# Spacing the bursts of partial-array products in a list-scheduled encoder layer

## The chip, the cores and the metric

One Trainium2 chip, one core. The metric is the device time of one execution in microseconds (us). The kernel before takes 2392.24 us, the median of 3 runs (2391.76 to 2394.51).

## The reference: what is computed

One layer of a bidirectional encoder, over two sequences (512 and 1024 tokens of 1024 channels), in float32:

```python
h = rms_norm(x, n_pre_mix); proj = h @ w_in            # 6672 columns
# Gated DeltaNet, 4 heads of 128, forward and backward
o_a = gated_delta_chunked(q, k, v, g[0], beta[0]) + flip(gated_delta_chunked(flip(q), ...))
# HGRN2, 4 heads of 128, forward and backward
o_b = gla_chunked(qh, kh[0], ih, logf[0]) + flip(gla_chunked(flip(qh), ...))
y_a = (rms_norm(o_a) * silu(z)) @ w_br_gdn;  y_b = (rms_norm(o_b) * silu(g)) @ w_br_hg
x = x + rms_norm((gates[0] * y_a + gates[1] * y_b) @ w_out, n_post_mix)
h2 = rms_norm(x, n_pre_ffn)
return x + rms_norm((silu(h2 @ w_gate) * (h2 @ w_up)) @ w_down, n_post_ffn)
```

Inside each chunk `gated_delta_chunked` solves a unit lower triangular system. The kernel forms the inverse of its matrix: 32x32 blocks first, then merged to 64x64 and to 128x128 by small products.

## The kernel before, in words

**Dense products.** Every large matrix product is done with 128x128 weights against 128x512 moving data. Each float32 operand is split into a high and a low part, and three products (high by high, high by low, low by high) are added in one PSUM bank. In the trace they are `MATMUL ... 128*128 128x512`, one instruction for the weights and one for the product.

**Partial-array products.** The merges of the triangular inverse (`merges` in `gdn_mix`, below `def pairs`) use quarters and halves of the array: 32x32 and 64x64 weights (`32*32 32x32`, `64*64 64x64` in the trace). They are plain float32, and each one becomes four instructions of the tensor engine: two weight loads and two products, so the trace has two `MATMUL` for one product of the program. For one head of the 1024-token sequence the merges are four bursts: 32 products of 32x32, a copy of their result, 48 products of 32x32, copies, 16 products of 64x64, a copy, 16 products of 64x64. For the 512-token sequence the bursts are half as long. HGRN2 has bursts of its own, with 128x32 weights.

**Who sets the order.** Nothing is issued as it is written. `Tape` records every instruction as an `Op` with a modelled duration (`cost`), `units` joins products of one form that follow each other into a unit (one burst above is one unit), and `schedule` then runs a list scheduler over the whole program: it keeps a modelled clock for each engine, holds a heap `future` of units whose operands come later and a heap `ready` of units that could start, and lets the engine with the earliest possible start take its ready unit of the lowest `prio` (its place in the written order). A unit whose PSUM bank is still read by another engine is put back into `future` with the time `w` at which it may start. `emit` then writes the instructions in the order found. [...] The name `form` is the shape of the weights for float32 products, `FULL` is (128, 128), and it is `None` for the dense products.

All recorded instructions go through one call, so all rows of the profile have the line of `emit` (L632 before, L649 in the changed kernel); the tiles' names tell them apart. `bank` is any PSUM bank; `ha_a` holds the split activations and `wa_a` the split weights of the dense products in the mixer part, `xr_a` those of the later part; `la_a`, `ba_a`, `sm_a` and `sa_a` hold the rest.

**Stages.** Projections, mixers and first part of the feed-forward are interleaved in about the first 1160 us. After that come dense products only.

Of the kernel before, what the change touches and what calls it, by code (L numbers as in the profile page):

```python
# [2 lines left out]

# [42 lines left out]
PO = False  # L46
NVEC = 88
AHEAD = {1: 1536, 3: 2064, 7: 4112 - 512}
TOKENS, NORMED = 14.0, 30.0
QSQ = P * EPS ** 0.5  # L50
EPSQ = P * EPS * EPS
# [109 lines left out]
class Tape:  # L161
# [11 lines left out]
    GROUP = 4  # L173
    AHEAD = 500
    RATE = 260.0
    SLACK = {"sync": 600, "vector": 100, "scalar": 100, "gpsimd": 100, "tensor": 100}

    class Eng:
# [252 lines left out]
    def schedule(self):  # L431


        self.units()
        ops = self.ops
        for o in ops:
            o.succ = []
            o.rel = 0.0
            o.asked = False
        npend = [0] * len(ops)  # L440
        for o in ops:
            for j in o.need:
                if ops[j].unit is not o.unit:
                    npend[o.unit[0].idx] += 1
                    ops[j].succ.append(o)
        pools = []
        for v in self.vts.values():
            if v.ops:
                v.left = len(v.ops)
                v.fin, v.use = {}, {}  # L450
                v.pool.tiles.append(v)
                if v.pool not in pools:
                    pools.append(v.pool)
        for p in pools:
            p.begin(len(ops), self.cuts)
        engs = list(self.ENGS)
        future = {e: [] for e in engs}
        ready = {e: [] for e in engs}
        clock = {e: 0.0 for e in engs}
        lanes = []  # L460
        start, turn = {}, {}
        far = []
        front = 0

        def lat(a, b):
            a, b = self.ENGS[a], self.ENGS[b]
            return self.LAT.get((b, a), 30 if a == b else 36)

        def ask(o):

            if o.idx > front + self.AHEAD:
                heapq.heappush(far, o.idx)
                return
            for x in o.unit:
                for v in x.tiles:
                    if v.at is None:
                        got = v.pool.take(v, front)
                        if got is None:
                            heapq.heappush(v.pool.queue, (o.prio, o.idx))
                            return  # L480
                        v.fin = {}
                        for f in got:
                            for e, t in f.items():
                                v.fin[e] = max(v.fin.get(e, 0.0), t)
                    for e, t in v.fin.items():
                        if v.left == len(v.ops):
                            o.rel = max(o.rel, t + lat(e, x.eng))
            heapq.heappush(future[o.eng], (o.rel, o.idx))

        def enable(o, t):  # L490
            o = o.unit[0]
            npend[o.idx] -= 1
            o.rel = max(o.rel, t)
            if npend[o.idx] == 0:
                ask(o)

        def retry(p):
            q, p.queue = p.queue, []
            while q:
                ask(ops[heapq.heappop(q)[1]])  # L500

        for o in ops:
            if o.unit[0] is o and npend[o.idx] == 0:
                ask(o)
        done = 0
        form = None
        wire = 0.0
        held = {"vector": 0.0, "gpsimd": 0.0}
        while done < len(ops):
            best = None  # L510
            for e in engs:
                t = clock[e]
                fu, re_ = future[e], ready[e]
                while fu and fu[0][0] <= t:
                    i = heapq.heappop(fu)[1]
                    heapq.heappush(re_, (ops[i].prio, i))
                if re_:
                    c = t
                elif fu:
                    c = fu[0][0]  # L520
                else:
                    continue
                if best is None or c < best[0]:
                    best = (c, e)
            assert best is not None, "no instruction can start"
            t, e = best
            fu, re_ = future[e], ready[e]
            while fu and fu[0][0] <= t:
                i = heapq.heappop(fu)[1]
                heapq.heappush(re_, (ops[i].prio, i))  # L530
            k = None
            if e == "tensor" and form == self.FULL:
                k = min((x for x in re_ if ops[x[1]].form == form and x[0] < re_[0][0] + self.NEAR), default=None)
            if k is None:
                k = heapq.heappop(re_)
            else:
                re_.remove(k)
                heapq.heapify(re_)
            o = ops[k[1]]
            w = t  # L540
            for x in o.unit:
                for v in x.tiles:
                    if v.pool.kind == "PSUM":
                        for b, f in v.use.items():
                            if b != e:
                                w = max(w, f + lat(b, e))
            if w > t:
                heapq.heappush(fu, (w, o.idx))
                continue
            if o.meth == "dma_start":  # L550
                if len(lanes) >= self.LANES:
                    t = max(t, lanes[-self.LANES])
                wire = max(wire, t + 1000) + o.form
                o.dur = max(o.dur + o.form, wire + 700 - t)
                lanes.append(t + o.dur)
            if e == "tensor":
                if o.form is not None and o.form != form:
                    t += self.ENTER if o.form == self.FULL else self.SWITCH
                form = o.form
            if o.port:  # L560
                w = max(0.0, held["gpsimd" if e == "vector" else "vector"] - t - o.port)
                o.dur += w
                o.occ += w
                held[e] = t + o.dur
            freed = []
            first = t
            for o in o.unit:
                start[o.idx] = (t, done)
                turn[o.idx] = (first, done)
                for v in o.tiles:  # L570
                    if v.pool.kind == "PSUM":
                        v.use[e] = t + o.dur
                done += 1
                clock[e] = t + o.occ
                fin = t + o.dur
                for s in o.succ:
                    if s.eng == e == "tensor":
                        enable(s, t + o.occ)
                    else:
                        enable(s, fin + lat(e, s.eng) + (self.SLACK[e] if e != s.eng else 0))  # L580
                for v in o.tiles:
                    if v.left == len(v.ops):
                        v.fin = {}
                    v.left -= 1
                    v.fin[e] = max(v.fin.get(e, 0.0), fin)
                    if v.left == 0:
                        v.pool.give(v)
                        if v.pool not in freed:
                            freed.append(v.pool)
                t += o.occ  # L590
            f0 = front
            while front < len(ops) and front in start:
                front += 1
            for p in freed:
                retry(p)
            if front > f0:
                while far and far[0] <= front + self.AHEAD:
                    ask(ops[heapq.heappop(far)])
                for p in pools:
                    if p not in freed and p.queue:  # L600
                        retry(p)
            elif freed:
                for p in pools:
                    if p not in freed and p.queue and any(s.waits for s in p.segs):
                        retry(p)
        self.span = max(clock.values())
        self.start = start
        return [ops[i] for i in sorted(turn, key=turn.get)]
# [139 lines left out]
def layer(ctx, tc, x_p, x_s, w_out, n_post_mix, n_post_ffn, w_down, vec, xt_p, xt_s, w_in, w_br, w_gate, w_up,  # L748
# [304 lines left out]
    def need(*keys):  # L1053
        def f():
            ts_ = [pl.done.get(k) for k in keys]
            return None if None in ts_ else max(ts_)
        return f
# [1169 lines left out]

    def pre_stream():
        yield from prelude(seqs[0])
        yield need(("inv", 0, 2))  # L2230
        yield from prelude(seqs[1])

    def gdn_stream():
# [244 lines left out]
    for _ in range(2):  # L2478
        t = pl.tile(hp, [P, KD * TB], F32R, "ring", "ring", 2)
# [122 lines left out]
```

## Time and profile before

| what | value |
|---|---|
| median of 3 runs | 2392.24 us (2391.76 to 2394.51) |
| the profiled execution's own time | 2393.4 us |
| its span | 2391.7 us |
| mean granted clock of the tensor engine | 0.997 |
| tensor engine, products (PE) | 2368.8 us busy, 99%, 14133 instructions |
| tensor engine, weight loads (PEld) | 1976.9 us busy, 14133 instructions |
| VectorE (DVE), ScalarE (ACT), GpSimd (POOL) | 72%, 52%, 31% busy |
| PE's instruction queue (q8) | 111 packets, 1.82 MB |

How to read it: times are in us from the start of the span. PE's busy time is a union of products whose ends are modelled, so a short gap between two products can stand as busy. What the tensor engine loses is better read from the starts in the timeline. `[2.50 <-issue]` behind a row is idle time ahead of it for which the trace shows no semaphore. In a table of windows, PEclk is the granted clock (1.00 is full speed) and (x11) the number of products that began there.

### The profile page before, as it was taken

To read this page: it belongs to the slowest core of one execution; us is meant where nothing else is said; L and a number is where in the kernel's file an instruction comes from. 1 tells how busy PE (TensorE), PEld (TensorE's weight loads), DVE (VectorE), ACT (ScalarE), POOL (GpSimd) and SP (SyncE) were. 2 spreads that over 40 slices of the span, in tenths; PEclk is the share of its full clock that TensorE was granted. 3 is DMA by queue.
4 is the path that set the end of the run, shared out by engine and by line. 5 is a ranking of instruction groups with operands and counts; after the bars stand their busy time and mean duration, and the time that the engine had idled before them with its cause. 6 is when DMAs were issued, how large, how long until landed. Compare 5 with 4: busy or idle time off the path is not lost.

```text
span 2391.7 us, 37849 instructions
## 1 busy us (share of the span) xinstructions
PE 2368.8 (99%) x14133; PEld 1976.9 (83%) x14133; DVE 1733.5 (72%) x2827; ACT 1241.0 (52%) x2158; POOL 752.6 (31%) x1019
## 2 busy tenths in 40 slices
PE   8999999999999999999999999999999999999998
PEld 6888888878888888888888888888888888888887
DVE  7787899848847959748866894755887878545566
ACT  6665876736636637547442464544353544433343
POOL 0623434231602602502310001113666764200221
PEclk9999999999999999999999999999999999999999
DMA  5241743321320231233874453552454544674463
GB/s 197 90 150 63 240 128 88 98 67 41 107 93 18 91 92 54 77 97 117 297 256 176 141 207 120 174 157 94 165 191 163 189 173 166 202 254 139 148 205 125
DMA packets 193495, 337.72 MB, mean 141 GB/s; under 512 B 53184, under 2 KB 92960, under 8 KB 193312
## 3 DMA queue, kind: packets, MB, share of 16 engines
q1 hardware_dynamic: 193312, 335.31, 42.3%
q8 instruction: 111, 1.82, 0.3%
q14 instruction: 72, 0.59, 0.1%
HBM read 254.59 MB, written 80.66 MB: 140 GB/s over the span
## 4 chain that ended last, share of the span: by engine, by line
PE 95%; DVE 3%; DMA 1%; issue 1%; ACT 0%; SPq 0%; POOL 0%; DVEq 0%; ACTq 0%; POOLq 0%
PE bank L632 95%; DVE la_a L632 1%; DMA la_a<-lay_w_in 1%; DVE ba_a L632 1%; DVE sm_a L632 0%; DVE wa_a L632 0%; SPq L632 0%; ACT wa_a L632 0%; ACT la_a L632 0%; ACT ba_a L632 0%; DMA dram_cr_sc<-sm_a 0%; DVE da_a L632 0%; DMA dram_u_sc<-la_a 0%; POOL sm_a L632 0%; DVE sa_a L632 0%
## 5 line engine op out<-in xcount | busy, mean ns | idle before, releaser
L632 PE MATMUL bank<-ha_a,wa_a 128*128 128x512 f32 x5424 | 1308.4, 395 | 0.1
L632 PEld LDWEIGHTS bank<-ha_a,wa_a 128*128 128x128 f32 x5424 | 1004.2, 188 | 203.4 <-issue 1.6
L632 PE MATMUL bank<-xr_a 128*128 128x512 f32 x1386 | 314.3, 389 | 0.0
L632 PEld LDWEIGHTS bank<-xr_a 128*128 128x128 f32 x1386 | 260.1, 188 | 54.0
L632 PE MATMUL bank<-xr_a,ha_a 128*128 128x512 f32 x1200 | 275.2, 389 | 0.0
L632 PEld LDWEIGHTS bank<-xr_a,ha_a 128*128 128x128 f32 x1200 | 225.2, 188 | 46.8
L632 POOL TENSOR_TENSOR ba_a<-ba_a 128x512 f32<-128x512 f32 (+1 forms) x129 | 168.7, 1315 | 229.4 <-ACT wa_a L632 86.7
L632 ACT ACTIVATE la_a<-la_a 128x512 f32<-128x512 f32 (+1 forms) x303 | 191.4, 648 | 60.5 <-DVE la_a L632 44.4
L632 ACT ACTIVATE wa_a<-la_a 128x1024 fp32r<-128x1024 f32 (+1 forms) x120 | 117.1, 983 | 129.1 <-PE bank L632 117.0
L632 DVE TENSOR_TENSOR wa_a<-la_a,wa_a 128x1024 fp32r<-128x1024 f32 (+1 forms) x120 | 141.8, 1189 | 51.5 <-PE bank L632 33.4
L632 DVE TENSOR_TENSOR wa_a<-ba_a,wa_a 128x1024 fp32r<-128x1024 f32 (+1 forms) x104 | 126.1, 1228 | 71.7 <-PE bank L632 50.4
L632 ACT ACTIVATE ha_a<-ba_a 128x512 fp32r<-128x512 f32 (+1 forms) x123 | 79.2, 646 | 138.5 <-PE bank L632 113.1
L632 POOL TENSOR_TENSOR sm_a<-la_a 128x28 f32<-128x28 f32 (+36 forms) x186 | 86.6, 466 | 203.2 <-DMA la_a<-dram_u_sc 151.6
L632 ACT ACTIVATE wa_a<-ba_a 128x1024 fp32r<-128x1024 f32 (+1 forms) x104 | 100.5, 984 | 85.5 <-PE bank L632 71.9
L632 DVE TENSOR_TENSOR ha_a<-ba_a,ha_a 128x512 fp32r<-128x512 f32 (+1 forms) x123 | 127.3, 1039 | 14.0 <-ACT ha_a L632 13.4
L632 DVE TENSOR_TENSOR la_a<-la_a 128x512 f32<-128x512 f32 (+2 forms) x182 | 125.5, 700 | 9.8 <-ACT la_a L632 8.2
L632 POOL TENSOR_TENSOR la_a<-la_a 128x256 f32<-128x256 f32 (+1 forms) x62 | 66.0, 1076 | 172.5 <-DVE la_a L632 86.6
L632 PE MATMUL bank<-wa_a,ha_a 128*128 128x512 f32 x528 | 120.1, 389 | 0.0
L632 ACT ACTIVATE ba_a<-ba_a 128x512 f32<-128x512 f32 (+1 forms) x172 | 109.9, 647 | 17.8 <-DVE ba_a L632 9.4
L632 DVE TENSOR_TENSOR xr_a<-da_a,xr_a 128x1024 fp32r<-128x1024 f32 (+2 forms) x60 | 71.1, 1199 | 64.1 <-ACT xr_a L632 44.0
L632 PEld LDWEIGHTS bank<-wa_a,ha_a 128*128 128x128 f32 x528 | 99.0, 188 | 20.5
L632 ACT ACTIVATE xr_a<-da_a 128x1024 fp32r<-128x1024 f32 (+2 forms) x60 | 58.6, 987 | 106.0 <-PE bank L632 105.0
(205 smaller groups left out, 3391.7 us busy)
## 6 DMA issues: line engine op xcount, KB each, us to landing
la_a<-lay_w_in SPq DMA_DIRECT2D x69, 512.0 KB
ba_a<-lay_w_in SPq DMA_DIRECT2D x35, 512.0 KB
ba_a<-lay_w_up SPq DMA_DIRECT2D x35, 512.0 KB
ba_a<-lay_w_gate SPq DMA_DIRECT2D x35, 512.0 KB
dram_a_sc<-xa_a SPq DMA_DIRECT2D x56, 256.0 KB
ba_a<-w_ffn_down SPq DMA_DIRECT2D x24, 512.0 KB
da_a<-dram_a_sc SPq DMA_DIRECT2D x22, 512.0 KB
ba_a<-dram_a_sc SPq DMA_DIRECT2D x20, 512.0 KB
```

What stands on the lines that cost most here:

```text
L632: f(*[m(a) for a in o.args], **{k: m(a) for k, a in o.kw.items()})
```

## The change

`schedule` keeps a queue `past` of what the tensor engine has been given: for each instruction group its modelled start and how many instructions it is (4 for a float32 product, 2 for a dense product or a transpose). Before a unit of partial-array products is given out, entries older than `FETCH` (5000 ns) are dropped, and the unit's instructions are added to those that are left. If they come to more than `BLOCK` (256; for a unit that is itself over 192 instructions, its own count and 64), the unit goes back into `future` with the time at which enough of the older entries will have passed out of the 5000 ns. No wait is put into the program: only the order found is another.

```diff
+    FETCH = 5000.0
+    BLOCK = 256
...
+        past = deque()
...
+            if e == "tensor" and o.form is not None and o.form != self.FULL:
+                n = 4 * len(o.unit)
+                while past and past[0][0] < t - self.FETCH:
+                    past.popleft()
+                n += sum(c for _, c in past) - max(self.BLOCK, n + 64)
+                for s, c in past:
+                    if n <= 0:
+                        break
+                    n -= c
+                    w = max(w, s + self.FETCH + 1)
             if w > t:
                 heapq.heappush(fu, (w, o.idx))
                 continue
...
+            if e == "tensor":
+                past.extend((t + i * o.occ, 4 if x.form is not None and x.meth == "matmul" else 2) for i, x in enumerate(o.unit))
...
+TRIG = 2
...
-        yield need(("inv", 0, 2))
+        yield need(("inv", 0, TRIG))
```

The last two hunks put a name in place of a number and change nothing.

The rows below are the tensor engine's order. A row is the line, the instruction, the tiles and the shape of the result, and xN how many products of the program stand in a row. The first place is head 0 of the 1024-token sequence, the end of its burst of 32 products of 32x32 and the start of its burst of 48. Before:

```order
L632 MATMUL bank_88<-la_a 32x32
L632 MATMUL bank_88<-la_a,ba_a 32x32
L632 MATMUL bank_89<-ha_a,wa_a 128x512 x6
L632 MATMUL bank_91<-la_a 32x32 x4
L632 MATMUL bank_93<-la_a 32x32 x2
```

The same place in the changed kernel:

```order
L649 MATMUL bank_88<-la_a 32x32
L649 MATMUL bank_88<-la_a,ba_a 32x32
L649 MATMUL bank_89<-ha_a,wa_a 128x512 x21
L649 MATMUL bank_94<-ha_a,wa_a 128x512
L649 MATMUL bank_91<-la_a 32x32 x4
L649 MATMUL bank_93<-la_a 32x32 x2
```

Between the two bursts stood 6 dense products, and now stand 22. These are the first rows of the tensor engine that differ. Heads 1, 2 and 3 had 5, 5 and 12 there and have 22 now.

The second place is the end of the burst of 48 in the same head and the start of its first 64x64 burst. Before:

```order
L632 MATMUL bank_91<-la_a 32x32 x4
L632 MATMUL bank_93<-la_a 32x32 x2
L632 MATMUL bank_89<-ha_a,wa_a 128x512 x11
L632 MATMUL bank_88<-la_a 64x64
L632 MATMUL bank_88<-la_a,ba_a 64x64
```

In the changed kernel:

```order
L649 MATMUL bank_91<-la_a 32x32 x4
L649 MATMUL bank_93<-la_a 32x32 x2
L649 MATMUL bank_94<-ha_a,wa_a 128x512 x18
L649 MATMUL bank_89<-la_a 64x64
L649 MATMUL bank_89<-la_a,ba_a 64x64
```

Here 11 dense products became 18; in heads 1 to 3 it was 10, 12 and 12 and is 18.

The third place is head 3, where the gap between the bursts of 32 and 48 was the widest before:

```order
L632 MATMUL bank_87<-ha_a,wa_a 128x512 x6
L632 MATMUL bank_90<-la_a 32x32 x32
L632 MATMUL bank_87<-ha_a,wa_a 128x512 x12
L632 MATMUL bank_90<-la_a 32x32 x4
L632 MATMUL bank_88<-la_a 32x32 x2
```

In the changed kernel:

```order
L649 MATMUL bank_90<-ha_a,wa_a 128x512 x6
L649 MATMUL bank_92<-la_a 32x32 x32
L649 MATMUL bank_90<-ha_a,wa_a 128x512 x18
L649 MATMUL bank_88<-ha_a,wa_a 128x512 x4
L649 MATMUL bank_92<-la_a 32x32 x4
L649 MATMUL bank_94<-la_a 32x32 x2
```

The 12 dense products became 22. The number of all products, and of the bursts (48 of them), is the same in both kernels. So is the number of dense products ahead of each 128x32 burst that follows these places: 2036, 2132, 2620, 2751, 3156, 3300, 3758 and 3806, before and after.

More of the change, by code (lines that the diff above doesn't have):

```diff
@@ L1 @@
 import heapq
+from collections import deque
 from contextlib import ExitStack, contextmanager
```

## The prediction

> **What bounds the kernel now.** I read the page first, then who the tensor engine waits for, then its timeline around the bursts, then tables of windows for the clock. The page:
>
> ```profile
> span 2391.7 us, 37849 instructions
> PE 2368.8 (99%) x14133; PEld 1976.9 (83%) x14133; DVE 1733.5 (72%) x2827; ACT 1241.0 (52%) x2158; POOL 752.6 (31%) x1019
> q8 instruction: 111, 1.82, 0.3%
> PE 95%; DVE 3%; DMA 1%; issue 1%; ACT 0%; SPq 0%; POOL 0%; DVEq 0%; ACTq 0%; POOLq 0%
> ```
>
> The products are 99% of the span and 95% of the chain that ended last, so only what shortens the tensor engine's own stream counts. The q8 row is its instruction queue: 1.82 MB in 111 packets is 16.4 KB each, and 2 x 14133 instructions over 111 packets is 255 instructions in each. So the stream comes in blocks of 256. What the engine waits for, over the whole span and then from 505 us on:
>
> ```profile
> PE bank L632 <- ACT la_a L632: 7.9, 2, 7.1
> PE bank L632 <- issue: 5.7, 3, 2.5
> PE bank L632 <- ACT wa_a L632: 1.1, 2, 0.6
> PE bank L632 <- DVE la_a L632: 0.8, 2, 0.5
> ...
> PE bank L632 <- issue: 5.7, 3, 2.5
> PE bank L632 <- ACT la_a L632: 0.8, 1, 0.8
> ```
>
> 7.1 us is the start of the program. The rest is 2.7 us of waits for data (0.8 us of it after 505 us) and three idle times of 5.7 us in all that no semaphore explains. The timeline of PE shows the three, each in the second burst of 32x32 products of a head of the long sequence; the first fence is head 0:
>
> ```profile
> 509.04 0.21 PE L632 MATMUL bank<-la_a 32*32 32x32 f32 x1
> ...
> 509.72 1.66 PE L632 MATMUL bank<-ha_a,wa_a 128*128 128x512 f32 x6
> 511.31 0.70 PE L632 MATMUL bank<-la_a 32*32 32x32 f32 x59
> 514.52 0.53 PE L632 MATMUL bank<-la_a 32*32 32x32 f32 x37 [2.50 <-issue]
> 514.98 4.35 PE L632 MATMUL bank<-ha_a,wa_a 128*128 128x512 f32 x11
> ...
> 664.95 1.42 PE L632 MATMUL bank<-ha_a,wa_a 128*128 128x512 f32 x5
> ...
> 668.57 0.21 PE L632 MATMUL bank<-la_a 32*32 32x32 f32 x1 [1.38 <-issue]
> 668.81 4.10 PE L632 MATMUL bank<-ha_a,wa_a 128*128 128x512 f32 x10
> ...
> 853.72 1.42 PE L632 MATMUL bank<-ha_a,wa_a 128*128 128x512 f32 x5
> ...
> 857.75 0.19 PE L632 MATMUL bank<-ba_a,la_a 32*32 32x32 f32 x1 [1.80 <-issue]
> ```
>
> In head 0 the engine stops in the middle of a burst, after 59 of 96 products, with the same operands before and after. If a block of instructions was missing, the stops must lie a whole number of blocks apart. Two windows from stop to stop:
>
> ```profile
> 514.50:668.50 154.00, 152.68 (x1271) 129.52 (x1271) 126.31 (x246) 96.03 (x182) 54.52 (x93) 0.99 0.27 80
> 668.50:857.70 189.20, 186.54 (x1403) 157.56 (x1404) 136.53 (x256) 103.70 (x198) 56.30 (x101) 0.99 0.22 68
> ```
>
> 1271 products and 1271 loads are 2542 instructions, 18 short of 10 blocks of 256; 1403 and 1404 are 2807, 9 short of 11 blocks. The missing few are semaphore instructions, which the table leaves out. I read the stops as waits for an instruction block. Head 3 has the same bursts and no stop:
>
> ```profile
> 1037.46 0.75 PE L632 MATMUL bank<-la_a 32*32 32x32 f32 x64
> 1038.14 3.02 PE L632 MATMUL bank<-ha_a,wa_a 128*128 128x512 f32 x12
> 1041.09 1.04 PE L632 MATMUL bank<-la_a 32*32 32x32 f32 x96
> ```
>
> There 12 dense products stand between the bursts, not 6 or 5. That is the change's own remedy at a smaller dose.
>
> The stops have a second price, in the granted clock. Windows around the stops (PE busy, then the other engines, granted clock third from the end):
>
> ```profile
> 512.46:515.87 3.41, 1.35 (x41) 1.17 (x42) 0.66 (x2) 0.79 (x1) 1.03 (x4) 1.00 0.20 73
> 515.87:519.29 3.42, 3.42 (x11) 2.18 (x9) 3.29 (x9) 0.02 (x1) 0.00 (x0) 0.50 0.00 0
> ...
> 666.06:669.47 3.41, 2.03 (x101) 1.54 (x100) 1.84 (x4) 1.61 (x3) 0.14 (x2) 1.00 1.04 353
> 669.47:672.89 3.42, 3.42 (x11) 2.18 (x9) 1.89 (x5) 0.00 (x0) 1.27 (x2) 0.50 0.81 175
> 853.79:857.20 3.41, 2.15 (x84) 1.56 (x85) 2.94 (x4) 0.00 (x0) 0.00 (x0) 1.00 0.52 211
> 857.20:860.62 3.42, 2.87 (x28) 2.38 (x28) 2.36 (x6) 1.96 (x3) 0.00 (x0) 1.00 0.30 71
> ```
>
> After a window of 3.41 us with 1.35 us or 2.03 us of products, the next one runs at 0.50; after 2.15 us it does not. The third stop is split over two windows and goes free.
>
> **The change part by part.** *The stops.* The listed idle counts from the modelled end of the product before, so I add one product's length:
>
> ```profile
> L632 PE MATMUL bank<-la_a 32*32 32x32 f32 x608 | 10.8, 196 | 4.1 <-issue 3.9 <-DVE la_a L632 0.3
> ```
>
> 2.50 + 1.38 + 1.80 + 3 x 0.196 = 6.27 us from start to start. Do they all go? The tightest is head 0: from its first burst's start (509.04) to the resumption (514.52) the missing block took 5.48 us. With 22 dense products at 0.227 us,
>
> ```profile
> 84.32 37.67 PE L632 MATMUL bank<-ha_a,wa_a 128*128 128x512 f32 x165
> ```
>
> ((37.67 - 0.39) / 164, with 0.39 us for the last one's length), the same product comes 0.68 (first burst, 509.72 - 509.04) + 22 x 0.227 + 0.11 (head 3's 3.02 us for 12 against 11 x 0.227 + 0.39, rounded) + 0.52 (59 products) = 6.3 us after that start, 0.8 us later than the block. Heads 1 and 2 needed about 4.3 and 4.7 us (668.57 - 664.95 + 0.68; 857.75 - 853.72 + 0.68). So all three go: -6.3 us. Bounds: one still there, 2.7 us; none.
>
> *The clock.* At 0.50 the 11 and 10 dense products took 4.35 and 4.10 us. Head 3's 12 took 3.02; 11 would take 2.79 and 10 would take 2.57. So 1.56 + 1.53 = 3.1 us go with the idle that caused them. Bounds: both stay, 0; both go, -3.1.
>
> [...]
>
> *The dense products moved.* 16, 17, 17 and 10 more stand ahead of the bursts of 48, and 7, 8, 6 and 6 more ahead of the first 64x64 bursts: 87 x 0.227 = 19.7 us of work that is done sooner and lacks later. Nothing is added, and its cover is that other dense products are ready when these are gone. The order says they are: each later 128x32 burst has the same number of dense products ahead of it. So 0 now, 19.7 us if the cover were gone.
>
> *Changes of form.* 48 bursts before and after, so as many entries and exits. Counted in the order, dense products alternate with 128x128 float32 products about 12 times more. Bounds each: 0 to 0.11 us (the return from a burst, above), so 0 to 1.3 us; since these keep the whole array, I take the low end, +0.1.
>
> *Waits for data.* From 505 us on PE waited 0.8 us for data. The new order could take that away or, at worst by the page, bring as much as the whole program had, 2.7 us. VectorE copies each burst's result before the next burst; with 22 dense products between (5.0 us) instead of 6, that copy has more time. The copy's readers, the 64x64 merges and the recurrence behind them, come up to 5 us later in a head; what waits behind them on PE is dense work that does not need them. I take 0.
>
> Sum against the profiled execution (2393.4 us, span 2391.7, 1.7 us outside): -6.3 - 3.1 + 0.1 = -9.3, span 2382.4, execution 2384.1. The median of the runs is 1.2 us under the profiled execution, so I subtract from the median: 2392.2 - 9.3 = **2383 us**, -0.39%.
>
> **The rivals.**
>
> (a) *The clock is not the stops' doing.* Small products fill little of the array, and the slow windows come from the bursts, which stay. For it: both windows hold bursts. Against it: a window full of bursts kept its clock, and so did head 3.
>
> ```profile
> 608.00:611.40 3.40, 3.40 (x138) 2.81 (x137) 3.40 (x7) 2.30 (x5) 2.63 (x6) 1.00 0.15 59
> ```
>
> Time: 2392.2 - 6.3 + 0.1 = 2386. [...]
>
> (b) *One stop returns.* The four extra semaphore instructions and the new order shift the block borders, and one burst meets one, with its slow window: 2383 + 2.7 + 1.5 = 2387. For it: the margin of 0.8 us. Against: the rule spaces by instruction count, wherever the border lies.
>
> (c) *The change doesn't do what it says.* The stops are not waits for instructions and return in the new order at the same products: 2392. Against it stand the whole numbers of blocks and head 3.
> [...]
>
> (d) *Slower.* The 87 dense products are missed later in the mixers: the recurrences of the last head end up to 5 us late, nothing dense is ready, and PE idles. It decides from the point where more than 9.3 us / 0.227 = 41 of them are missed. All 87: 2383 + 19.7 = 2403. Against it: 0.8 us of waits for data in all of the mixers after 505 us, and the unchanged counts ahead of later bursts.
>
> **How the numbers follow.** Forecast, 2381 to 2385.5: 0.65. (a) 0.13. (b) 0.09. (c) 0.08. (d) 0.05. A change under 0.2% (4.8 us) can't be told from none here, so faster means under 2387.4. That takes the forecast, (a) and about half of (b), 0.82; same is the other half of (b), (c) and a little of (d), 0.14; slower 0.04. The range takes in (a) and (b), the bounds of alternation and waits (+1.3, +2.7, -0.8), and leaves (c) and (d) out: 2380 to 2388.5.
>
> **What would show it.** Right: no idle `<-issue` on PE in the second bursts of the four heads; granted clock 1.00 in all windows around them (mean above 0.997); PE busy for about 9 us less; waits for data still 2 to 4 us; 22 and 18 dense products between bursts in the timeline. Clock wrong: slow windows without stops. Stops misread: idle `<-issue` again, not a whole number of blocks apart. Cover wrong: PE waits for DVE or ACT, or for POOL's inverse, between 520 and 1160 us.

## The result, and the profile after

The changed kernel takes 2388.11 us (median of 17 runs, 2385.86 to 2389.97) against 2392.58 for the kernel before beside it (17 runs). The ratio is 0.9982, with a 95% interval of 0.9974 to 0.9989. That is 4.3 us less by the ratio and 4.5 by the medians, where 9.3 were forecast. The direction holds and the interval lies below 1, but the size is under half, and it lies within the 0.2% that the prediction took as not to be told from no change. In the profiled executions it is 2389.0 us against 2393.4, span 2387.3 against 2391.7, so 4.4 us.

The page of the changed kernel, the lines that answer to those shown of before:

```profile
span 2387.3 us, 37828 instructions
PE 2367.1 (99%) x14133; PEld 1975.4 (83%) x14133; DVE 1727.1 (72%) x2827; ACT 1239.1 (52%) x2158; POOL 750.5 (31%) x1019
q8 instruction: 111, 1.82, 0.3%
```

The products and the instruction packets are the same in number. The timeline of PE in head 0 (start, length, then instruction, operands, shapes, count):

```profile
509.86 5.29 PE L649 MATMUL bank<-ha_a,wa_a 128*128 128x512 f32 x22
515.08 1.05 PE L649 MATMUL bank<-la_a 32*32 32x32 f32 x96
516.05 4.38 PE L649 MATMUL bank<-ha_a,wa_a 128*128 128x512 f32 x18
```

There are 22 and 18 dense products around the second burst, and its 96 products run without a break. The same windows of time that held the first stop, and then the half clock:

```profile
512.46:515.87 3.41, 3.41 (x104) 2.67 (x103) 0.36 (x1) 1.14 (x2) 0.85 (x1) 1.00 0.19 77
515.87:519.29 3.42, 3.42 (x40) 2.84 (x27) 3.00 (x8) 3.42 (x6) 0.14 (x2) 1.00 0.02 5
```

Both are full of products, at a granted clock of 1.00. So the two large terms of the forecast were collected. What was given back stands in the list of PE's waits from 505 us on, in which before had 5.7 us of `issue` and 0.8 us of waits for data:

```profile
PE bank L649 <- DVE la_a L649: 1.5, 2, 1.3
PE bank L649 <- ACT la_a L649: 0.9, 1, 0.9
PE bank L649 <- ACT ba_a L649: 0.8, 1, 0.8
PE bank L649 <- ACT wa_a L649: 0.5, 2, 0.2
PE bank L649 <- DVE sm_a L649: 0.2, 1, 0.2
```

`issue` is gone, and 0.8 us of waits for data have become 3.9 us, in seven waits. One of the seven, 0.9 us for ScalarE at 830.30, is the wait that before had at 836.52; the other six are new. A table of windows shows where. First before, then the changed kernel; the second number is the window's length and the third PE's busy time:

```profile
500.00:700.00 200.00, 196.12 (x1667) 165.09 (x1666) 145.93 (x284) 111.93 (x210) 61.51 (x108) 0.98 0.31 90
700.00:900.00 200.00, 197.37 (x1498) 168.31 (x1497) 143.41 (x278) 110.39 (x213) 57.14 (x98) 1.00 0.20 60
900.00:1160.00 260.00, 260.00 (x2021) 220.87 (x2020) 199.80 (x381) 159.71 (x291) 67.08 (x113) 1.00 0.32 102
1160.00:1700.00 540.00, 540.00 (x2450) 449.17 (x2450) 371.55 (x533) 241.79 (x386) 103.88 (x83) 1.00 0.52 175
```

```profile
500.00:700.00 200.00, 199.62 (x1705) 169.19 (x1704) 150.22 (x292) 113.15 (x216) 59.06 (x110) 1.00 0.32 91
700.00:900.00 200.00, 199.14 (x1507) 170.07 (x1506) 149.59 (x290) 114.17 (x219) 60.84 (x104) 1.00 0.21 60
900.00:1160.00 260.00, 259.19 (x2025) 220.59 (x2024) 191.17 (x364) 157.89 (x286) 69.64 (x109) 1.00 0.35 115
1160.00:1700.00 540.00, 538.25 (x2420) 445.68 (x2419) 365.73 (x535) 238.58 (x385) 96.78 (x81) 1.00 0.51 172
```

Up to 900 us, the idle time in these tables falls from 6.51 to 1.24 us. From 900 to 1700 us, where before had none, it rises to 2.56 us. So most of the loss lies far behind the last burst that was moved, at about 1040 us.

The largest of the new waits is at the handover from the branch products (`ha_a,wa_a`) to the w_out product (`wa_a,ha_a`). The timeline of PE there, and below it that of VectorE:

```profile
1317.73 1.47 PE L649 MATMUL bank<-sa_a,la_a 128*128 128x128 f32 x12
1319.04 0.60 PE L649 MATMUL bank<-sa_a,ba_a 128*128 128x128 f32 x4
1319.47 1.91 PE L649 MATMUL bank<-sa_a,la_a 128*128 128x128 f32 x16
1322.67 2.52 PE L649 MATMUL bank<-wa_a,ha_a 128*128 128x512 f32 x10 [1.29 <-DVE la_a L649]
```

```profile
1315.20 0.69 DVE L649 TENSOR_TENSOR ba_a<-bank,ba_a 128x512 f32<-128x512 f32 x1 [2.03 <-PE bank L649]
...
1317.70 1.22 DVE L649 TENSOR_TENSOR wa_a<-ba_a,wa_a 128x1024 fp32r<-128x1024 f32 x1 [0.67 <-PE bank L649]
1318.84 0.68 DVE L649 TENSOR_TENSOR ba_a<-bank,ba_a 128x512 f32<-128x512 f32 x1
1319.44 0.68 DVE L649 TENSOR_TENSOR ba_a<-la_a 128x512 f32<-128x512 f32 x1
...
1321.84 1.28 DVE L649 TENSOR_TENSOR la_a<-bank,sa_a 128x512 f32<-128x512 f32 x2
```

The 32 transposes of x2 (12 + 4 + 16, four to a bank) fill all eight banks that the kernel has. The w_out product needs one back, and VectorE empties the first only at 1321.84. Until 1317.70 VectorE itself waited for PE (2.03 and 0.67 us); from then on it has no gap. From the first of the last 16 transposes to the product, 3.20 us pass.

### The profile page after: what moved, and what is told of

It is laid out like the page before. It is cut to its first block, busy times and chain, and to the rows that moved or that the text cites. A ratio compares the mean times of both kernels' runs of the same rounds, so it can differ in the third digit from the quotient of the medians.

```text
span 2387.3 us, 37828 instructions
## 1 busy us (share of the span) xinstructions
PE 2367.1 (99%) x14133; PEld 1975.4 (83%) x14133; DVE 1727.1 (72%) x2827; ACT 1239.1 (52%) x2158; POOL 750.5 (31%) x1019
## 4 chain that ended last, share of the span: by engine, by line
PE 93%; DVE 3%; ACT 1%; DMA 1%; issue 1%; POOL 0%; SPq 0%; DVEq 0%; POOLq 0%; ACTq 0%
PE bank L649 93%; DVE la_a L649 2%; DVE ba_a L649 1%; DMA la_a<-lay_w_in 1%; ACT la_a L649 1%; DVE wa_a L649 0%; ACT ba_a L649 0%; ACT wa_a L649 0%; DMA ba_a<-lay_w_in 0%; DVE sm_a L649 0%; DMA dram_g_sc<-la_a 0%; POOL la_a L649 0%; SPq L649 0%; DVE da_a L649 0%; DMA dram_u_sc<-la_a 0%
## 5 line engine op out<-in xcount | busy, mean ns | idle before, releaser
L649 DVE TENSOR_TENSOR wa_a<-ba_a,wa_a 128x1024 fp32r<-128x1024 f32 (+1 forms) x100 | 118.1, 1196 | 78.7 <-PE bank L649 34.9
L649 ACT ACTIVATE wa_a<-la_a 128x1024 fp32r<-128x1024 f32 (+1 forms) x124 | 122.7, 998 | 99.2 <-PE bank L649 96.6
L649 ACT ACTIVATE wa_a<-ba_a 128x1024 fp32r<-128x1024 f32 (+1 forms) x100 | 94.8, 964 | 125.5 <-PE bank L649 116.3
L649 DVE TENSOR_TENSOR la_a<-la_a 128x512 f32<-128x512 f32 (+2 forms) x158 | 108.8, 701 | 10.6 <-ACT la_a L649 10.1
L649 POOL TENSOR_TENSOR la_a<-la_a,sm_a 128x30 f32<-128x30 f32 (+39 forms) x217 | 107.8, 497 | 16.2
```

Source lines behind the costliest of these rows:

```text
L649: f(*[m(a) for a in o.args], **{k: m(a) for k, a in o.kw.items()})
```

## The experiments

Two theories were set against each other at the start. A: the stops are waits for a block of 256 instructions and the half clock follows the idle, so both go whenever the border is moved out of the bursts; what the change gives back comes from the new order. Rivals: the bursts themselves slow the clock; the spacing as such costs time.

**Moving the block borders without a new order.** The order of before is kept, and the first four products of each of the eight early 32x32 bursts are issued twice (the second writes the same numbers over the first, so nothing is left out):

```diff
         for o in order:
             f = getattr(getattr(self.nc, o.eng), o.meth)
-            f(*[m(a) for a in o.args], **{k: m(a) for k, a in o.kw.items()})
+            twice = o.form == (32, 32) and len(o.unit) <= 24 and o.unit.index(o) < 4
+            for _ in range(1 + twice):
+                f(*[m(a) for a in o.args], **{k: m(a) for k, a in o.kw.items()})
```

> The kernel before with its order untouched on every engine; only 32 of the early 32x32 products (four in each of the eight 32x32 bursts of the short sequence) are issued twice, which puts 128 more instructions ahead and so moves all later block borders by half a block, out of the second bursts of the long sequence's heads. Theory A (the stops are missing instruction blocks, and the gain that failed to come was lost to waits for data that the new order brought): no stop in the four heads (at most 1 us in all elsewhere), clock at 1.00 throughout, PE's waits for data after 505 us as before, 0.8 us; 0.7 us more for the products issued twice; time 8 to 9 us under before, about 2384. Theory B (the stops belong to these products or their operands, and spacing helped in another way): stops at the same products, time as before or 0.7 us more.

Measured: 2385.22 us, ratio 0.9969 (0.9957 to 0.998), 7.5 us less than before (8 to 9 were expected), with 128 instructions more. PE's waits over the whole span of this kernel:

```profile
PE bank L634 <- ACT la_a L634: 7.1, 1, 7.1
PE bank L634 <- issue: 0.8, 1, 0.8
PE bank L634 <- ACT wa_a L634: 0.7, 2, 0.5
PE bank L634 <- DVE la_a L634: 0.4, 1, 0.4
```

None of these lies behind 505 us; the 0.8 us of `issue` stand at 421.65, early in the program, where before had no `issue`. The spacing was not needed for the gain: the position of the border was enough, and it was worth more than the change.

**The borders moved further.** The same with seven products instead of four (`< 7`), 224 instructions in all:

> As the run above, but seven products of each early burst are issued twice, 224 more instructions. The borders now lie so that in all four heads a block is asked for shortly ahead of the second burst and needed in it; by the durations of before 2.5, 1.2, 1.4 and 1.8 us lie between in heads 0 to 3. Theory A: a stop in each of the four heads, head 3 for the first time, each of 1.3 to 4 us, 8 to 14 us in all; two to four slow windows of the clock; time 3 to 10 us over before. Theory B: the three stops as before and none in head 3, time 1.2 us over before.

Measured: 2394.44 us, ratio 1.0004 (0.9995 to 1.0013). The stops are back, 5.4 us of them: 0.92 in head 0, 2.75 in head 1, 1.74 in head 2, none in head 3, where one was expected, and the time stayed under the 3 to 10 us more that was expected. Head 0 of this kernel:

```profile
511.32 0.84 PE L634 MATMUL bank<-la_a 32*32 32x32 f32 x75
513.07 0.33 PE L634 MATMUL bank<-la_a 32*32 32x32 f32 x21 [0.92 <-issue]
```

Before, the stop came after 59 products of this burst, here after 75. With 224 instructions ahead of it, the next border lies 256 - 224 = 32 instructions later, which is 16 products with their loads: 59 + 16 = 75. That fixes the border to the instruction.

The packed traces settle it for every stop. They hold each packet of the instruction queue q8 (16384 bytes, one block) and each instruction of the tensor engine, semaphore instructions included. In the profiles of before, of the changed kernel and of the twelve experiments, 16 idle times of PE are listed as `issue`. Each of them ends when 193 or 194 instructions beyond a whole number of 256 have begun, and 1.24 to 1.60 us after a packet of q8 has ended; for the three stops of before it is 1.31, 1.47 and 1.27 us. In all these profiles no block of instructions begins sooner than 1.24 us after its packet (1546 blocks). So every stop is a wait for an instruction block, the one at 421.65 too. The packets also show how little is fetched ahead: the packet of a block starts between 4.8 us before and 6.0 us after the engine enters the block ahead of it.

**Other spacings.** The changed kernel with `FETCH = 3000.0` (13 dense products between the bursts instead of 22) and with `FETCH = 4000.0` (17):

```diff
-    FETCH = 5000.0
+    FETCH = 3000.0
```

> The changed kernel with 3000 ns in place of 5000, so that 13 dense products stand between the bursts of 32 and 48 instead of 22. Theory A: the block of head 0, which took 5.5 us, is needed after 0.68 + 13 x 0.227 + 0.11 + 0.52 = 4.3 us, so a stop of up to 1.2 us there, up to 0.5 us in heads 1 and 2, none in head 3; waits for data other than in the changed kernel, at other products, since the order is another: 1 to 5 us after 505 us. Theory C (the waits for data come from delaying the bursts): clearly fewer than in the changed kernel, in proportion to 13 against 22.

> The changed kernel with 4000 ns in place of 5000: 17 dense products between the bursts. Theory A: head 0's block is needed after 5.2 us, so a stop of at most 0.3 us; none elsewhere; waits for data after 505 us of 1 to 5 us at other products than in the changed kernel, not ordered by the spacing. Theory C: waits for data between those with 13 and those with 22.

Measured: 2395.69 us, ratio 1.0012 (1.0004 to 1.0021), and 2393.28 us, ratio 1.0006 (0.9996 to 1.0015). Both lose the whole gain. At 4000 three stops are left, 2.6 us in all, where at most 0.3 us was expected: one in head 0, 0.71 us at 680.91 in the second 64x64 burst of head 1, and 0.89 us at 1145.01. The one in head 0:

```profile
514.28 0.65 PE L649 MATMUL bank<-la_a 32*32 32x32 f32 x48 [1.02 <-issue]
```

It comes after 96 - 48 = 48 products. The 11 more dense products ahead are 22 instructions, so the border lies 11 products earlier than before: 59 - 11 = 48, again to the instruction. At 3000 no stop is listed, although its margin was smaller still. The time that a block takes is not constant: in head 0 the packet ended 2.9 us after the engine had entered the block ahead at 3000, 4.2 us after it before, and 5.0 us after it at 4000. The rest of the loss is waits for data. From 505 us on they are 6.9 us at 3000 and 4.0 us at 4000; the changed kernel has 3.9 us in the profile above and 2.2 us in a second one. At 3000, a timeline row and two windows:

```profile
1336.93 8.29 PE L649 MATMUL bank<-wa_a,ha_a 128*128 128x512 f32 x28 [4.02 <-ACT ha_a L649]
```

```profile
1333.80:1337.20 3.40, 0.27 (x1) 0.27 (x2) 3.40 (x5) 1.64 (x2) 0.00 (x0) 1.00 0.30 108
1337.20:1340.60 3.40, 3.40 (x10) 2.66 (x10) 3.40 (x4) 1.06 (x1) 0.00 (x0) 0.59 0.62 205
```

At 4000 the same place costs 3.3 us. So the theory that waits grow with the spacing falls. And a low granted clock, 0.59 in the second window, follows this wait too, in a stage with no burst at all: it belongs to the idle.

**The borders moved from the very start.** The order of before, with 28 products of 32x32 of the identity in the first 7 us, written to a bank that nobody reads there (112 instructions):

```diff
             f(*[m(a) for a in o.args], **{k: m(a) for k, a in o.kw.items()})
+            if o.meth == "affine_select" and o.args[0] is self.lead:
+                i32 = self.real(self.lead)[0:32, 0:32]
+                for _ in range(28):
+                    self.nc.tensor.matmul(self.spare[0:32, 0:32], i32, i32, start=True, stop=True)
...
+    nc.lead, nc.spare = ident, real[bank, 7]
```

> The kernel before with its order untouched; 28 added 32x32 products of the identity (112 instructions) stand ahead of everything else, in the first 7 us, in which PE waits for data anyway, and write a part of a PSUM bank that nothing reads. They move every block border by 112 instructions at no cost in time. Theory A: no stop in the four heads, full clock, waits for data as before (0.8 us after 505 us); time 0.5 to 1 us under the kernel that issued early products twice, 2384 to 2385, and 3 to 5 us under the changed kernel. Theory B (the stops belong to these products): as before.

Measured: 2384.64 us (2383.75 to 2386.33), ratio 0.9967 (0.9956 to 0.9979), 8.6 us less than before and 3.5 less than the changed kernel. From 505 us on PE waits 0.9 us in all:

```profile
PE bank L632 <- ACT la_a L632: 0.7, 1, 0.7
PE bank L632 <- DVE wa_a L632: 0.2, 1, 0.2
```

**Another order without spacing.** The kernel of the first experiment, with a rule of the scheduler that has nothing to do with bursts set otherwise (`NEAR`, 300 to 280):

```diff
-    NEAR = 300
+    NEAR = 280
```

> No spacing. The kernel with 32 early products issued twice (so no stops), and one number of the list scheduler changed from 300 to 280: how far down the written order PE may look for a product of full form. The order is the same up to about 600 us and another behind it, though no burst is delayed. Theory A (any new order brings waits for data, the order before happens to have few): waits for data on PE of 2 to 6 us between 600 and 1500 us, time 2387 to 2391. Theory C (they come from delaying the bursts): under 1.5 us, time about 2385.

Measured: 2389.61 us, ratio 0.9991 (0.9981 to 1.0001), 4.4 us over the first experiment. Its waits from 505 us on:

```profile
PE bank L634 <- DVE wa_a L634: 1.1, 2, 0.6
PE bank L634 <- ACT wa_a L634: 0.5, 2, 0.2
PE bank L634 <- DVE la_a L634: 0.4, 1, 0.4
PE bank L634 <- issue: 0.3, 1, 0.3
```

A new order costs waits even where no burst is spaced. In its starts, product to product, the losses lie near 646, 670, 1161, 1164, 1322 and 1416 us and add up to 3.9 us: partly the places of the changed kernel. The one at 670 is the stop of 0.3 us in the list; the others are waits for data, where the first experiment had none behind 505 us. So a new order as such is enough to bring such waits; no run shows that the distance between bursts adds any of its own.

**The changed kernel with the early products.** Spacing and 112 instructions together, one profile:

> The changed kernel with the same 28 products ahead of everything, order untouched. Theory A: with the bursts spaced the place of the borders doesn't matter: no stop in the four heads, waits for data as in the changed kernel, time within 2 us of it. If the changed kernel only owed its lack of stops to where its borders fell, stops of 1 to 3 us come back.

Measured: 2387.56 us in the one run. No stop in the four heads, wherever the borders lie, and the wait at the handover is there. The spacing does what it says; it is not what a border happens to do. Beside the fifth experiment (2384.64 us), which has the same early products and the old order, this run also gives the price of the new order where neither has a stop in the four heads: 2.9 us, from one run.

**The wait near 1321, three attempts.** The first put the six sums of VectorE that open the w_out product later in the written order:

```diff
+            with nc.sooner(-150):
-            tt(sums[i], a21, a22, ALU.add)
-            tt(a21, a11, a21, ALU.subtract)
-            tt(a11, sums[i], a11, ALU.subtract)
+                tt(sums[i], a21, a22, ALU.add)
+                tt(a21, a11, a21, ALU.subtract)
+                tt(a11, sums[i], a11, ALU.subtract)
```

> The changed kernel, with the six sums on VectorE that open the product with w_out put 150 places later in the written order. These stood on VectorE ahead of the evictions that PE waited for at 1321 us (1.5 us). Theory A (that wait is VectorE's order at this place): it goes; the order behind about 1300 us is another, with waits of its own of 0 to 4 us. Time 2385 to 2390.

Measured: 2395.53 us, ratio 1.0014 (1.0004 to 1.0023). A miss: the wait stayed (1.35 us), and a new one of 4.53 us for `ha_a` came at 1338.44. The four sums that stand ahead of the banks in VectorE's queue were still there: they are the last sums of the merges, not those that were moved.

The second took work off VectorE, by giving the eight subtractions for the low part of h2 to GpSimd, which is idle there (0.00 us busy from 1320 to 1340 us):

```diff
-                split(hi[:, ks, cs], lo[:, ks, cs], t4(x2_cols(xs[i], i)))
+                split(hi[:, ks, cs], lo[:, ks, cs], t4(x2_cols(xs[i], i)), nc.gpsimd)
```

> The changed kernel, with the eight subtractions that make the low part of the transposed h2 (h2_of's splits, 128x512 each) moved from VectorE to GpSimd, which has nothing to do between 1320 and 1340 us; nothing is left out. Theory A' (after the spacing TensorE reaches the handover from the merges to the w_out product when VectorE is full, so what it lacks there is VectorE's time): VectorE has less to do there, the wait of 1.3 to 1.5 us near 1321 goes, and the time is 1 to 2 us under the changed kernel's, near 2386.5; the smaller waits near 527, 645, 1124 and 1416 us stay. Rival (the wait is for a bank or a product that no split holds up): the wait stays at 1.3 us or more, and the time is the changed kernel's within 0.7 us. If GpSimd's subtractions come late for the products of the low parts, a new wait of over 1 us follows before 1345.

> The changed kernel again, on the same chip as the run beside it, as its measure. Every theory: 2387.5 to 2389.5, waits after 505 us near 3.9 us in the listed waits, the one near 1321 among them.

Measured: 2387.43 us (ratio 0.9977, 0.9968 to 0.9986), beside 2387.85 us for the changed kernel itself on the same chip (0.9979, 0.9969 to 0.9989). The wait stayed at 1.29 us in both. The second profile of the changed kernel lists 2.2 us of waits for data from 505 us on, not the 3.9 us that were expected: the waits for ScalarE at 830 and 1125 us are missing, so these two come and go between executions of one kernel, while those at 528, 646, 1321 and 1416 us stand in both. The timelines say why the first theory of this place failed here: the first of the moved subtractions comes at 1323.17, behind the wait. What it can free, it frees too late, and the rival's numbers came out.

The same move in the kernel with the early products, where no wait was to be removed:

> The order of before with 112 instructions ahead (the experiment that had no stop and no wait over 0.7 us after 505), with the eight subtractions on GpSimd as well; nothing is left out. Theory A': there TensorE waits for nothing at the handover, so taking work off VectorE buys nothing: 2384 to 2385.5, no wait near 1321. Rival (VectorE's load holds TensorE back there in a way that the waits don't list): 1 to 2 us under 2384.6.

Measured: 2384.07 us (ratio 0.9967, 0.9955 to 0.9978), no measurable difference from 2384.64, as expected.

The third changed VectorE's queue alone: the two multiplications that empty the first banks are put ahead of the four last merge sums.

```diff
+        i = next(n for n, o in enumerate(order) if o.eng == "vector" and o.args[0].tensor.name.endswith("_hgn"))
+        j = [n for n in range(i) if order[n].eng == "vector"][-4]
+        order[j:i + 2] = order[i:i + 2] + order[j:i]
         for o in order:
```

> The changed kernel with one thing moved in VectorE's queue, nowhere else: the first two multiplications that empty banks of transposed x2 (2 x 128x512, at 1321.84 in the changed kernel) stand ahead of the four last sums of the merges (ba_a<-la_a to la_a<-ba_a, 1319.44 to 1321.24) instead of behind them; nothing is left out. Theory A'' (the 32 transposes fill all eight banks, so TensorE's next product waits until VectorE empties the first one, and VectorE comes to it 2.4 us late, because the sums stand ahead of it in its queue): the wait of 1.29 us near 1321 goes, to under 0.3 us, and TensorE's next product starts some 1.5 us sooner after its transposes; the time is 1 to 2 us under the changed kernel's, near 2386.5. Rival (TensorE waits for VectorE's last merge sums, or for operands that the sums make): the wait stays or grows by the 1.2 us by which the sums are put back.

Measured: 2388.29 us, ratio 0.9983 (0.9973 to 0.9992). The timeline of PE, and below it that of VectorE:

```profile
1319.72 1.91 PE L653 MATMUL bank<-sa_a,la_a 128*128 128x128 f32 x16
1321.38 3.90 PE L653 MATMUL bank<-wa_a,ha_a 128*128 128x512 f32 x16
1326.36 18.98 PE L653 MATMUL bank<-wa_a,ha_a 128*128 128x512 f32 x82 [1.08 <-DVE la_a L653]
```

```profile
1319.68 1.28 DVE L653 TENSOR_TENSOR la_a<-bank,sa_a 128x512 f32<-128x512 f32 x2
1320.88 0.68 DVE L653 TENSOR_TENSOR ba_a<-la_a 128x512 f32<-128x512 f32 x1
...
1325.62 0.68 DVE L653 TENSOR_TENSOR la_a<-bank,sa_a 128x512 f32<-128x512 f32 x1
```

Half of the expectation held: the product starts 1.66 us after the first of the 16 transposes instead of 3.20 us, so the wait was for the bank, and it cost 1.5 us. But the time did not measurably move, because the wait came back as 1.08 us at the next bank, which VectorE now empties at 1325.62. The order within VectorE's queue moves this wait; it does not remove it. From 1317.94 to 1326 us VectorE has no gap there, so its work is more than fits ahead of the banks. In the first experiment the last 24 transposes start at 1316.77 and the product follows without a wait:

```profile
1316.77 2.78 PE L634 MATMUL bank<-sa_a,la_a 128*128 128x128 f32 x24
1319.31 5.96 PE L634 MATMUL bank<-wa_a,ha_a 128*128 128x512 f32 x25
```

There VectorE began to empty banks at 1317.44, and three of its 128x512 sums stand at 1312.17 already, ahead of the transposes. So it came to the handover with less left to do. Which decision of the scheduler, 800 us earlier, leads to this is not settled.

## Why the prediction was right and wrong

**The stops, -6.3: right.** All three are gone, and so they are in the first and fifth experiments, by another road. The borders were found again twice at the product that the count of instructions gives (75 and 48). Counted with the semaphore instructions, the three stops lie 2560 and 2815 instructions apart: 10 blocks, and 11 blocks less one record. In the working for head 0 the 0.11 us is 0.13 by its own figures; nothing hangs on it. One sign was misread: "PE busy for about 9 us less" could not show the stops, which are idle time, and busy time fell by 1.7 us only (2368.8 to 2367.1).

**The clock, -3.1: right for the profiled execution.** Both windows run at 1.00 now. Rival (a), the bursts slow the clock, falls: the bursts are still there, and at a spacing of 3000 a wait for data with no burst near it is followed by 0.59. The two windows at 0.50 went with the stops that left 1.35 and 2.03 us of products in the window ahead. What the prediction overlooked is that this price differs between executions of the kernel before. In the 93 that ran beside the experiments, the 37 with a mean granted clock of 0.999 or 1.000 took 2390.6 us in the mean, the 21 with 0.998 took 2392.8, and the 35 with 0.996 or 0.997 took 2395.8; all 17 of the changed kernel have 0.999 or 1.000. So 3.1 us from one profile was too much to take off a median: an estimate from these means is 2.0 us (2392.6 - 2390.6).

**The dense products moved, 0, and rival (d): right that they are not missed.** The change is not slower, and the places of the large waits are handovers, where PE waits for a bank or for an operand.

**Changes of form, +0.1.** No run separates this term.

**Waits for data, 0: wrong, and the step that failed.** The prediction took 0 here, with 2.7 us as the worst. What the new order cost can be read at points at which both kernels have done exactly the same products: the starts of the 1388th, 2621st, 3301st, 3807th, 4401st, 4601st, 5001st and last dense product, where the counts by shape agree. The table says how many us a kernel is ahead of before there. (The fifth experiment has its early products besides.)

| time in before, us | 421.0 | 790.1 | 992.9 | 1147.9 | 1288.6 | 1337.5 | 1428.1 | 1688.9 |
|---|---|---|---|---|---|---|---|---|
| changed kernel, the profile above | -0.9 | 6.3 | 8.2 | 7.4 | 7.1 | 5.6 | 4.4 | 4.4 |
| changed kernel, second profile | -0.9 | 6.3 | 9.1 | 9.4 | 8.5 | 7.0 | 5.7 | 5.8 |
| fifth experiment, the old order without stops | -0.9 | 7.0 | 9.1 | 9.1 | 8.7 | 8.7 | 8.7 | 8.7 |

At 421 us the order is still that of before, so the 0.9 us there are not the spacing's doing. From there to 993 us the changed kernel gains 9.1 and 10.0 us, so the two large terms, 9.4 us together, came in. Then, up to 1428 us, it gives back 3.8 us in one profile and 3.4 in the other, the old order under 0.5. That is the term that the prediction put at nothing. At the handover near 1321 us 1.5 us are lost in both profiles (3.20 - 1.66 = 1.54 us from start to start, against 1.29 listed), at 1416 and 1417 us 0.8 us, and at 1125 us 1.0 us in the first profile alone; the rest is in small losses that are not assigned.

The reasoning looked only at the bursts and their readers, and found that copies get more time. It took the 0.8 us of the old order as what any order would have. But the order behind the first moved burst is another, and these losses come 85 to 380 us behind the last spaced burst (at 1040). The sign named under "cover wrong" was nearly right in its engines, VectorE and ScalarE, but its place, 520 to 1160 us, was too narrow. Why the list scheduler lays these places out worse in the new order stays open.

**Rival (b), one stop returns: not in the bursts.** None did in the four heads. But the spacing does not cover every border: in the second profile of the changed kernel 0.48 us of `issue` stand at 1141.44, and in the last experiment 0.65 us at 1142.77, at the same product. It belongs to a group of 128x128 float32 products, a form that the rule does not hold back.

**Rival (c), the change does not do what it says: no.** All stops are waits for instruction blocks: at the 16 places counted above the instruction waited for its block and not for a semaphore, and went on 1.24 to 1.60 us after the block's packet had ended. In the profile of before such a wait is listed at three of the 111 packets, 5.7 us in all, and at no other; 112 early instructions brought 8.6 us.

**The range** (2380 to 2388.5) held the time by luck: it reached that far because rivals (a) and (b) had been let in, and the mechanism behind 2388.1 was neither.

## What to carry to other kernels

A stop that no semaphore explains can be tested cheaply: count the instructions between the stops, and shift the instruction stream by half a block with a few harmless instructions ahead, and see whether it moves by the count (here 224 instructions moved head 0's stop from product 59 to product 75). Where the order of a tuned list schedule is changed early, the waits behind it can all change, so the waits of the old order are no estimate for the new one: here the profiles of the old order list 0 to 0.9 us from 505 us on, and those of five other orders 2.0 to 9.1 us. Here a shift that keeps the order (2384.6 us) beat the rule that spaces the bursts (2388.1 us), but it holds only for this stream: 224 instructions instead of 112 or 128 brought the stops back, 5.4 us of them.

## What the runs showed of the hardware that was not expected

The eight subtractions that went to GpSimd took 2.0 us each, and while they ran most of VectorE's sums of two SBUF tiles grew longer, while its reads of PSUM did not. Groups of VectorE between 1322 and 1342 us, of the changed kernel and then with GpSimd at work (count, busy, mean ns):

```profile
L649 DVE TENSOR_TENSOR la_a<-bank,sa_a 128x512 f32<-128x512 f32 x8 | 5.0, 684 | 0.0
L649 DVE TENSOR_TENSOR ba_a<-ba_a 128x1024 f32<-128x1024 f32 x2 | 2.5, 1226 | 0.0
```

```profile
L649 DVE TENSOR_TENSOR la_a<-bank,sa_a 128x512 f32<-128x512 f32 x8 | 5.0, 682 | 0.0
L649 DVE TENSOR_TENSOR ba_a<-ba_a 128x1024 f32<-128x1024 f32 x2 | 4.4, 2204 | 0.1
```

The sum of two tiles went from 1226 to 2204 ns; one sum of this size that began at 1327.60 still took 1.24 us. So eight subtractions of 0.69 us, 5.1 us in all, were moved off VectorE, and its busy time between 1320 and 1340 us is still 19.70 us, against 20.00 and 19.20 us in the two profiles of the changed kernel. Why a sum grows is not shown.
